# The first attention's softmax: a maximum on VectorE, a bias on GpSimd, and an exponential that reads PSUM

## The chip, the cores and the metric

The kernel runs on one core of one Trainium2 chip. The metric is the device time of one execution in microseconds (us). The core has a matrix engine (TensorE, PE in the profile; its weight loads are PEld), VectorE (DVE), ScalarE (ACT), GpSimd (POOL) and SyncE (SP), which issues most DMAs. Each engine has its own queue and works through it in order; semaphores make one wait for another. TensorE writes its results into PSUM, a small memory of eight banks of 128x512 float32; VectorE and ScalarE read it there, and the other tiles live in SBUF.

## The reference, cut to what matters

The program is an encoder of two layers over 512 tokens of width 1024. The first layer has two groups of eight attention heads, A (grouped queries, width 64) and B (latent attention, width 64 + 32), then an output projection and an MLP. The second layer has a neighbourhood attention and an MLP. The change is in the softmax of the first layer alone:

```python
sc = jnp.einsum('bkgqd,bksd->bkgqs', qblk, kt).astype(jnp.float32) * scale
p = jax.nn.softmax(sc, axis=-1).astype(vt.dtype)
return jnp.einsum('bkgqs,bksd->bkgqd', p, vt)
```

For each head and each block of 128 queries this is a tile of 128x512 scores: scale, subtract the largest of each row, exponentiate, divide by the row's sum, multiply by the values. The scale holds the per-query norm of A's and B's queries too, so it is one number per row (per partition).

## The kernel before

All matrix products are made of float32r parts: a value is split into a high part (ScalarE copies it with rounding) and a low part (VectorE or GpSimd subtracts the high part), and two or three matmuls of the parts are added up in PSUM. So each matmul of a weight costs a ScalarE copy and a VectorE subtraction as well (`chunk`, L202 and L212 and L222), and so does each result that is used again (`split`, L830 and L833; `split_g`, L507 and L508).

The first attention is `attend` (from L961). It goes over 16 heads (8 of A, then two groups of 4 of B) and over 4 query blocks in each, 64 score tiles in all. For one tile, `scores` (L993 and on) does this:

- It takes one of the two PSUM banks of the tag `s` (`sbk`) and issues two matmuls (A) or three (B) into it (L997).
- L1001, VectorE: one custom instruction reads the scores from the bank, adds zero, multiplies by a negative scale, writes the result to the SBUF tile `p`, and keeps the minimum of each row in the tiny tile `t`. A second short instruction reads that accumulator out. Then the bank is free.
- L1003, ScalarE: the exponential of minus `p` plus that minimum, in place in `p`, with the row's sum kept (again a second instruction reads the accumulator out).
- L1004, VectorE: the reciprocal of the sum.
- L1005, GpSimd: `p` times the reciprocal.

Three tiles later `transpose` turns `p` with four TensorE transposes into a PSUM bank `t` (L972), ScalarE copies the high part out (L974) and VectorE the low part (L975). When two query blocks of a head are there, `values` multiplies them with the head's values into the bank `o` (L985), and `fold` adds the halves of the result (L946 on ScalarE, L949 on VectorE). `p` has five buffers, `t` (the tiny tile) six, and the banks `s` and `t` two each.

Beside the heads `step` feeds other work into the program (`fill`): the input projection's later columns (L501 to L503 on TensorE), the projections of B, and the first half of the output projection. Their helpers use GpSimd for low parts (L202) and for the rotary products (L562, L563).

The scales are prepared once: `q_scales` (L707 and on) makes `scA` for A, and `latents` makes `scB` for B (L816).

The order in which the instructions of this part stand in the engines' queues is not written out by hand. A planner takes the program's order as a priority, estimates each instruction's duration and the moment at which its inputs and buffers are there, and sorts the queues. Only a few places hold the program's order (`keep_in_program_order`, `fixed_order` in the second layer). So a changed instruction can change the order of others.

Of the kernel before, what the change touches and what calls it, by code (L numbers as in the profile page):

```python
# [11 lines left out]
AF = mybir.ActivationFunctionType  # L12
ALU = mybir.AluOpType
AX = mybir.AxisListType
PSUM = bass.MemoryType.PSUM

S = 512
D = 1024
P = 128
# [11 lines left out]
def f32(ap):  # L31
    return ap.bitcast(F32)
# [3 lines left out]
def encoder_kernel(ctx: ExitStack, tc: tile.TileContext, ins, out, dbg=None):  # L36
    nc = tc.nc
    PE, ACT, DVE, POOL, SP = nc.tensor, nc.scalar, nc.vector, nc.gpsimd, nc.sync
# [22 lines left out]
    def nm(s):  # L61
        cnt[0] += 1
        return f"{s}_{cnt[0]}"
# [18 lines left out]
    def sbk():  # L82
        return bank("s", 2)

    def stb():
        return bank("t", 2)

    def ob():
        return bank("o", 1)
# [4 lines left out]
    def tiny(n, dt=F32):  # L94
        return tp.tile([P, n], dt, tag=f"ti{n}", name=nm("ti"))

    def keep(shape, dt, name):
        return big.tile(shape, dt, tag=name, name=name)
# [9 lines left out]
    zeros = keep([P, 1], F32, "zeros")  # L108
# [362 lines left out]
    class Fill:  # L471
# [8 lines left out]
        def step(self):  # L480
            try:
                self.credit -= next(self.q[0][1])
            except StopIteration:
                self.q.pop(0)
# [42 lines left out]
    def bcast_cols(col_ap, nparts, bk):  # L527

        for i in range(4):
            PE.transpose(bk[0:nparts, i * P : (i + 1) * P], col_ap(i), ident)  # L530
# [38 lines left out]
    def stats_to_tok(bk, n, name):  # L569

        st = scratch()
        ACT.activation(st[0:n, :], bk[0:n, :], AF.Copy)
        tb = stb()
        for i in range(4):
            PE.transpose(tb[:, i * n : (i + 1) * n], st[0:n, i * P : (i + 1) * P], ident[0:n, 0:n])
        v = keep([P, 4 * n], F32, name)
        v3 = v.rearrange("p (i n) -> p i n", i=4)
        DVE.tensor_tensor(v3, tb[:, 0 : 4 * n].rearrange("p (i n) -> p i n", i=4),
                          r0sq.unsqueeze(2).to_broadcast([P, 4, n]), op=ALU.mult)
        DVE.tensor_scalar(v, v, 1.0, EPS, op0=ALU.mult, op1=ALU.add)  # L580
        y = rsqrt(v, 4 * n)
        DVE.tensor_tensor(v3, y.rearrange("p (i n) -> p i n", i=4),
                          r0.unsqueeze(2).to_broadcast([P, 4, n]), op=ALU.mult)
        return v3
# [17 lines left out]
    def ind2(t):  # L602
        return cst[:, C_I2 + 2 * t : C_I2 + 2 * t + 2]
# [103 lines left out]
    def q_scales():  # L707
        rs = stats_to_tok(hold["stq"], 8, "rsQ")
        sc = keep([P, 4, 8], F32, "scA")
        DVE.tensor_scalar(sc, rs, -0.125, 1.0, op0=ALU.mult, op1=ALU.mult)  # L710
        hold["scA"] = sc


# [46 lines left out]
    for m in range(6):  # L760
# [9 lines left out]
        else:  # L770
            ev_q(m - 2, banks[m])
    q_scales()
    rope_q(0)

# [32 lines left out]
    def latents():  # L807

        b = stb()
        for z in range(2):  # L810
            PE.matmul(b[0:2, :], ind2(z), sqs[z].t[:, 0:512], start=z == 0, stop=z == 1)
        sB = stats_to_tok(b, 2, "rsB")
        for z in range(2):
            sqs[z].free()
        scB = keep([P, 4], F32, "scB")
        DVE.tensor_scalar(scB, sB[:, :, 0], -(96.0 ** -0.5), 1.0, op0=ALU.mult, op1=ALU.mult)  # L816
        bk = stb()
        bcast_cols(lambda i: sB[:, i, 1:2].to_broadcast([P, P]), P, bk)
        hold["skvb"] = Slot(F32)
        ACT.activation(hold["skvb"].t[:, 0:512], bk, AF.Copy)  # L820
        hold["sB"], hold["scB"] = sB, scB
        for s_ in X:
            s_.free()
        yield 1.5
# [116 lines left out]
    def fold(o, e):  # L941

        if e == 0:
            hold["pair"] = scratch()
        a, c, pair = 64 * e, scratch(), hold["pair"]
        ACT.activation(c[0:64, :], o[64:128, :], AF.Copy)  # L946

        def add():
            DVE.tensor_tensor(pair[a : a + 64, :], o[0:64, :], c[0:64, :], op=ALU.add)  # L949
            if e:  # L950
                O.append(Slot())
                soon_a(lambda o=O[-1]: split(pair, o.pair()))

        soon(add)
# [6 lines left out]
    def attend(heads, step):  # L961


        late_t, late_v = [], []

        def transpose(h, i, p):
            if i % 2 == 0:
                h["pt"] = Slot(), Slot()
            h3, l3 = (s_.t.rearrange("p (k q) -> p k q", k=4)[:, :, (i % 2) * P : (i % 2 + 1) * P] for s_ in h["pt"])
            tb = stb()  # L970
            for k in range(4):
                PE.transpose(tb[:, k * P : (k + 1) * P], p[:, k * P : (k + 1) * P], ident)  # L972
            t3 = tb.rearrange("p (k q) -> p k q", k=4)
            ACT.activation(h3, t3, AF.Copy)  # L974
            DVE.tensor_tensor(l3, t3, f32(h3), op=ALU.subtract)  # L975
            if i % 2:
                late_v.append((h, i // 2, h["pt"]))

        def values(h, half, pt):
            if half == 0:  # L980
                h["o"] = ob()
            o = h["o"]
            for k in range(4):
                for n, m in enumerate(pt):
                    PE.matmul(o[:, 256 * half : 256 * half + 256], h["vlhs"](k), m.t[:, 256 * k : 256 * k + 256],  # L985
                              start=k == 0 and n == 0, stop=k == 3 and n == 1, skip_group_check=True)
            for s_ in pt:
                s_.free()
            if half:
                fold(o, h["e"])  # L990
                h["after"]()

        def scores(h, i):  # L993
            s = sbk()
            pl = h["passes"](i)
            for n, (lh, rh) in enumerate(pl):
                PE.matmul(s, lh, rh, start=n == 0, stop=n == len(pl) - 1)  # L997
            h["done"](i)
            t = tiny(4)
            p = pp.tile([P, 512], F32, tag="p", name=nm("p"))  # L1000
            DVE.tensor_tensor_reduce(p, s, zeros.to_broadcast([P, S]), op0=ALU.add, op1=ALU.min, scale=h["scale"](i),  # L1001
                                     scalar=3e38, accum_out=t[:, 1:2])
            ACT.activation(p, p, AF.Exp, bias=t[:, 1:2], scale=-1.0, accum_out=t[:, 2:3])  # L1003
            DVE.reciprocal(t[:, 3:4], t[:, 2:3])  # L1004
            POOL.tensor_scalar(p, p, t[:, 3:4], 1.0, op0=ALU.mult, op1=ALU.mult)  # L1005
            return p

        for h in heads:
            for i in range(4):
                ripe = list(late_v)  # L1010
                p = scores(h, i)
                if len(late_t) == 3:
                    transpose(*late_t.pop(0))
                late_t.append((h, i, p))
                if ripe:
                    values(*late_v.pop(0))
                step(h, i)
        for x in late_t:
            transpose(*x)
            while late_v:  # L1020
                values(*late_v.pop(0))
            fill.run(1.5)
# [68 lines left out]
    fill.add("z", product(w_in, 0, XP, tiles(1152, 256), ev_ckv, three, eng=POOL))  # L1091
    fill.add("z", rotary_key())
    fill.add("z", latents())
    projB(0, False)
    attend(all_heads(), step)
# [633 lines left out]
```

## Time and profile before

| What | us |
|---|---|
| median of three runs | 1184.7 |
| the three runs | 1185.4, 1184.7, 1183.35 |
| span of the profiled execution, first to last instruction | 1184.0 |
| PE busy in the span | 1160.5 (98%) |
| VectorE busy | 883.2 (75%) |
| ScalarE busy | 640.3 (54%) |
| GpSimd busy | 526.1 (44%) |

The time of the profiled execution itself is its span; the runs were timed apart from it. The mean granted clock of TensorE is 0.994 of full speed.

How to read the views. A row of instructions gives the line of the kernel, the engine, the operation, the tiles written and read, their shapes and how many there are; then busy time in us and the mean length of one in ns; then the idle time of the engine just before them, and which instruction's end stopped it. In the timeline a row begins with its start and its length in us, and a bracket gives the idle time before it and what ended it. In the waits a row says which instruction waited for which: us in total, times, the longest. The chain of work that ended last is followed back from the last instruction of the program: at each step to what released it, or to the instruction ahead of it on its engine.

### The profile page before, as it was taken

Reading aid. Unit: us, or ns where it says so; the run is one execution under the profiler, and the core shown is the slowest. Engines: PE = TensorE matmul, PEld = TensorE weight load, DVE = VectorE, ACT = ScalarE, POOL = GpSimd, SP = SyncE. Lnnn points to the kernel's source line nnn. Section 1 sums busy time; section 2 is a strip of 40 time slices with the busy share of each in tenths; the row PEclk is TensorE's granted clock in tenths of the full one; section 3 lists DMA queues with packets and bytes.
Section 4 is the critical chain, followed back from the end, with each engine's and each line's share of the span. In section 5 each row is a group of like instructions: output and inputs, shape, how many; then the busy total and the mean of one; then the engine's idle time right before and its main releaser. Section 6 shows DMA issues by size and latency. Waiting matters only on the chain.

```text
span 1184.0 us, 19784 instructions
## 1 busy us (share of the span) xinstructions
PE 1160.5 (98%) x7128; PEld 1021.2 (86%) x7128; DVE 883.2 (75%) x1514; ACT 640.3 (54%) x1081; POOL 526.1 (44%) x662
## 2 busy tenths in 40 slices
PE   9989999999999999999999999999999999999997
PEld 8667778888899899988998998988889989998895
DVE  5788998878967368786884676667996736778975
ACT  4468676664546247562553565555554624666344
POOL 3267343224562377819602232231376625774710
PEclk9999999999999999999999999999999999999998
DMA  7223225212524723225226464433352341322412
GB/s 244 71 54 92 68 78 134 62 56 77 167 86 134 263 70 90 72 90 165 67 72 178 131 184 126 116 112 109 107 165 76 115 134 55 98 64 89 143 36 71
DMA packets 110145, 128.01 MB, mean 108 GB/s; under 512 B 9075, under 2 KB 86816, under 8 KB 110048
## 3 DMA queue, kind: packets, MB, share of 16 engines
q1 hardware_dynamic: 106992, 119.30, 33.5%
q0 software_dynamic: 2304, 6.31, 2.2%
q8 instruction: 56, 0.92, 0.3%
q10 hardware_dynamic: 752, 1.15, 0.3%
q14 instruction: 41, 0.34, 0.1%
HBM read 104.32 MB, written 6.29 MB: 93 GB/s over the span
## 4 chain that ended last, share of the span: by engine, by line
PE 81%; DVE 4%; ACT 1%; issue 1%; POOL 0%; DVEq 0%; ACTq 0%
PE mm L503 8%; PE mm L501 8%; PE mm L502 8%; PE mm L390 4%; PE mm L389 4%; PE mm L388 4%; PE t L388 3%; PE t L389 3%; PE t L390 3%; PE s L502 2%; PE s L503 2%; PE s L501 2%; PE s L390 2%; PE s L388 2%; PE s L389 2%; PE s L997 2%
## 5 line engine op out<-in xcount | busy, mean ns | idle before, releaser
L309 DVE TENSOR_TENSOR wlo<-a,whi 128x896 fp32r<-128x896 f32 x132 | 161.8, 1230 | 83.7 <-ACT whi L308 82.9
L308 ACT ACTIVATE whi<-a 128x896 fp32r<-128x896 f32 x132 | 125.0, 950 | 155.0 <-PE o L502 45.8
L501 PE MATMUL mm<-a,whi 128*128 128x512 f32 x485 | 195.9, 406 | 0.9 <-DVE a L915 0.7
L503 PE MATMUL mm<-a,wlo 128*128 128x512 f32 x485 | 192.1, 397 | 2.5 <-DVE wlo L202 2.5
L502 PE MATMUL mm<-a,whi 128*128 128x512 f32 x485 | 192.5, 397 | 0.1
L202 DVE TENSOR_TENSOR wlo<-raw,whi 128x1024 fp32r<-128x1024 f32 (+4 forms) x117 | 139.3, 1193 | 66.4 <-ACT whi L212 63.9
L212 ACT ACTIVATE whi<-raw 128x1024 fp32r<-128x1024 f32 (+3 forms) x120 | 116.4, 971 | 92.2 <-PE s L502 39.8
L302 POOL TENSOR_TENSOR a<-a 128x128 f32<-128x128 f32 x132 | 85.1, 645 | 173.3 <-DMA a<-in_ffn_w_up_dram 103.9
L303 POOL TENSOR_TENSOR a<-a 128x256 f32<-128x256 f32 x132 | 120.2, 910 | 10.3
L304 POOL TENSOR_TENSOR a<-a 128x128 f32<-128x128 f32 x132 | 115.1, 872 | 10.3
L503 PEld LDWEIGHTS mm<-a,wlo 128*128 128x128 f32 x485 | 91.7, 189 | 23.7 <-DVE wlo L202 3.4
L501 PEld LDWEIGHTS mm<-a,whi 128*128 128x128 f32 x485 | 91.8, 189 | 20.4 <-PE t L972 0.9
L502 PEld LDWEIGHTS mm<-a,whi 128*128 128x128 f32 x485 | 91.9, 190 | 17.4 <-DVE a L545 0.4
L388 PE MATMUL mm<-a,whi 128*128 128x256 f32 x370 | 103.9, 281 | 0.0
L389 PE MATMUL mm<-a,whi 128*128 128x256 f32 x370 | 103.9, 281 | 0.0
L390 PE MATMUL mm<-a,wlo 128*128 128x256 f32 x370 | 103.7, 280 | 0.0
L1005 POOL TENSOR_SCALAR p<-p,ti 128x512 f32<-128x512 f32 x64 | 46.2, 724 | 92.3 <-DVE ti L1004 81.1
L1430 POOL TENSOR_SCALAR p<-p,ti 128x256 f32<-128x256 f32 x64 | 35.6, 567 | 104.8 <-DVE ti L1429 91.8
L388 PE MATMUL t<-a,whi 128*128 128x256 f32 x264 | 74.2, 281 | 0.0
L389 PE MATMUL t<-a,whi 128*128 128x256 f32 x264 | 74.1, 281 | 0.0
L390 PE MATMUL t<-a,wlo 128*128 128x256 f32 x264 | 73.9, 280 | 0.0
L390 PEld LDWEIGHTS mm<-a,wlo 128*128 128x128 f32 x370 | 69.6, 188 | 0.2 <-DVE wlo L309 0.2
(338 smaller groups left out, 3210.8 us busy)
## 6 DMA issues: line engine op xcount, KB each, us to landing
a<-in_ffn_w_up_dram SPq DMA_DIRECT2D x104, 256.0 KB
raw<-in_ffn_w_down_dram SPq DMA_DIRECT2D x46, 512.0 KB
raw<-in_od_w_qkv_dram SPq DMA_DIRECT2D x64, 128.0 KB
a<-in_ffn_w_down_dram SPq DMA_DIRECT2D x28, 256.0 KB
raw<-in_ffn_w_up_dram SPq DMA_DIRECT2D x12, 512.0 KB
raw<-in_ev_w_in_dram SPq DMA_DIRECT2D x12, 384.0 KB
a<-a SPq DMA_DIRECT2D x18, 256.0 KB
bias<-bx SPq DMA_DIRECT2D x16, 256.0 KB
```

The lines of the kernel that those rows point to most:

```text
L202: z = lambda: (eng or DVE).tensor_tensor(to, src, f32(high), op=ALU.subtract)
L212: ACT.activation(hi[:, 0:m], raw[:, 0:m], AF.Copy)
L303: POOL.tensor_tensor(r[:, 4:6], r[:, 2:3].to_broadcast([P, 2, P]), r[:, 0:7:6], op=ALU.add)
L304: POOL.tensor_tensor(r[:, 7], r[:, 3], r[:, 5], op=ALU.subtract)
L308: ACT.activation(hi[:, 0:896], raw[:, 128:1024], AF.Copy)
L309: DVE.tensor_tensor(lo[:, 0:896], raw[:, 128:1024], f32(hi[:, 0:896]), op=ALU.subtract)
L388: PE.matmul(o, wh, x[:, 0], start=kp == 0 and n in (0, 1, 3, 5), stop=False, skip_group_check=True)
L389: PE.matmul(o, wh, x[:, 1], start=False, stop=False, skip_group_check=True)
L390: PE.matmul(o, wl, x[:, 0], start=False, stop=kp == self.np - 1, skip_group_check=True)
L501: PE.matmul(o, wh, xh, start=first, stop=False)
L502: PE.matmul(o, wh, xl, start=False, stop=False)
L503: PE.matmul(o, wl, xh, start=False, stop=last)
```

## The change

VectorE only takes the maximum of each row of scores, straight from the bank. GpSimd multiplies it by the scale and by minus one, which gives the bias. ScalarE then reads the scores from the bank, and its instruction takes the scale and the bias as two operands per partition. The scales lose their minus sign, because the exponential now takes them as they are. `p` is first written by ScalarE. The bank is last read by ScalarE. The tile `zeros` is no longer read here.

```diff
@@ q_scales
-        DVE.tensor_scalar(sc, rs, -0.125, 1.0, op0=ALU.mult, op1=ALU.mult)
+        DVE.tensor_scalar(sc, rs, 0.125, 1.0, op0=ALU.mult, op1=ALU.mult)
@@ latents
-        DVE.tensor_scalar(scB, sB[:, :, 0], -(96.0 ** -0.5), 1.0, op0=ALU.mult, op1=ALU.mult)
+        DVE.tensor_scalar(scB, sB[:, :, 0], 96.0 ** -0.5, 1.0, op0=ALU.mult, op1=ALU.mult)
@@ scores
             t = tiny(4)
             p = pp.tile([P, 512], F32, tag="p", name=nm("p"))
-            DVE.tensor_tensor_reduce(p, s, zeros.to_broadcast([P, S]), op0=ALU.add, op1=ALU.min, scale=h["scale"](i),
-                                     scalar=3e38, accum_out=t[:, 1:2])
-            ACT.activation(p, p, AF.Exp, bias=t[:, 1:2], scale=-1.0, accum_out=t[:, 2:3])
+            DVE.tensor_reduce(t[:, 0:1], s, axis=AX.X, op=ALU.max)
+            POOL.tensor_scalar(t[:, 1:2], t[:, 0:1], h["scale"](i), -1.0, op0=ALU.mult, op1=ALU.mult)
+            ACT.activation(p, s, AF.Exp, bias=t[:, 1:2], scale=h["scale"](i), accum_out=t[:, 2:3])
             DVE.reciprocal(t[:, 3:4], t[:, 2:3])
             POOL.tensor_scalar(p, p, t[:, 3:4], 1.0, op0=ALU.mult, op1=ALU.mult)
             return p
```

## The prediction

> **What bounds the kernel now.** I read the page first (the span, the chain that ended last), then the busy time in 20 us stretches to find the part that the change touches, then the chain inside that part, and last the waits there.
>
> ```profile
> span 1184.0 us, 19784 instructions
> ...
> PE 81%; DVE 4%; ACT 1%; issue 1%; POOL 0%; DVEq 0%; ACTq 0%
> ```
>
> The chain is TensorE (PE) nearly all the way. The 64 score tiles of the first attention run from 73.8 us to the last scaling at 244.3 us (rows below), and only there can the change act. In the stretches, the fields are length, PE, weight load, VectorE (DVE), ScalarE (ACT), GpSimd (POOL), each in us and count, then granted clock, DMA share and GB/s:
>
> ```profile
> 70.00:90.00 20.00, 17.59 (x90) 13.70 (x88) 16.89 (x46) 15.18 (x32) 10.02 (x13) 0.91 0.18 47
> 90.00:110.00 20.00, 19.10 (x116) 15.83 (x116) 17.16 (x44) 16.20 (x38) 15.39 (x18) 1.00 0.35 100
> 130.00:150.00 20.00, 19.01 (x125) 16.46 (x125) 18.26 (x44) 17.13 (x36) 5.01 (x7) 1.00 0.33 74
> 150.00:170.00 20.00, 18.88 (x115) 16.02 (x116) 18.49 (x46) 15.38 (x35) 9.12 (x12) 1.00 0.29 76
> 190.00:210.00 20.00, 20.00 (x122) 17.15 (x121) 16.76 (x38) 12.79 (x28) 3.34 (x4) 1.00 0.63 168
> ```
>
> The reader sees two halves. From 190 us PE is busy without a gap: nothing that only relieves VectorE can pay there. Up to 170 us PE is idle for 1 to 2.4 us in each 20, and VectorE is at 17 to 18.5 of 20. The chain, from 140 us on (start, us, what), shows VectorE as the engine that ends last there:
>
> ```profile
> 144.09 0.66 DVE p L1001
> 144.75 0.01 DVE ti L1001
> 144.75 0.60 DVE a L975
> 145.36 0.60 DVE a L830
> ```
>
> So in this stretch a shorter VectorE instruction counts, but by little: L1001 takes 0.66 us of the queue, its neighbours 0.60.
>
> **The change, part by part.** Durations, from the groups of instructions between 68 and 250 us by form (busy us, mean ns, idle before); then a group of the whole trace, and two lines by themselves (shortest/median/longest ns, first and last start):
>
> ```profile
> L1005 POOL TENSOR_SCALAR p<-p,ti 128x512 f32<-128x512 f32 x64 | 46.2, 724 | 92.3 <-DVE ti L1004 81.1 <-DVE ti L166 4.1 <-PE s L997 3.6
> L1003 ACT ACTIVATE p<-p,ti 128x512 f32<-128x512 f32 x64 | 46.1, 720 | 12.2 <-DVE ti L1001 11.6
> L1001 DVE CUSTOM_DVE_ANT_0 p<-s,zeros,scB 128x512 f32<-128x512 f32 x32 | 23.7, 744 | 3.4 <-PE s L997 2.9 <-POOL p L1005 0.3
> L202 POOL TENSOR_TENSOR wlo<-raw,whi 128x512 fp32r<-128x512 f32 x9 | 12.7, 1409 | 5.2 <-ACT whi L222 4.1 <-ACT whi L212 1.1
> L833 ACT ACTIVATE a<-sc 128x512 fp32r<-128x512 f32 x13 | 8.2, 627 | 3.2 <-DVE sc L949 1.3 <-DVE sc L566 0.9 <-DVE sc L881 0.9
> L1001 DVE DVE_READ_ACCUMULATOR2_ANT ti<- 128x1 f32 x64 | 5.3, 83 | 0.0
> L507 ACT ACTIVATE a<-mm,gT 128x512 fp32r<-128x512 f32 x5 | 3.4, 681 | 0.0
> L833 ACT ACTIVATE a<-mm 128x512 fp32r<-128x512 f32 x4 | 2.4, 595 | 0.0
> ```
>
> ```profile
> L546 DVE COPY hT<-t 128x512 f32<-128x512 f32 x8 | 5.5, 682 | 0.0
> ```
>
> ```profile
> L1005 POOL TENSOR_SCALAR p<-p,ti x64: 688/696/1653, 77.6 to 244.3; 128x512 f32<-128x512 f32 x64
> ```
>
> ```profile
> L1430 POOL TENSOR_SCALAR p<-p,ti x64: 471/482/1697, 641.8 to 808.1; 128x256 f32<-128x256 f32 x64
> ```
>
> *VectorE.* 64 custom reductions (744 ns, with an 83 ns accumulator read each) go, 64 maxima over a 128x512 tile in PSUM come. No plain reduction stands in this trace. The nearest row is the copy out of PSUM of the same shape, 682 ns (L546); the bounds are 595 ns (the ScalarE copy out of PSUM) and 827 (744 + 83, if a maximum also needs its accumulator read). I take 682. In the queue, where instructions overlap a little, that is the step from 0.66 to the 0.60 us of L975: 0.06 us a tile, 64 x 0.06 = 3.8 us of VectorE in all. At 64 tiles in 171 us about 25 lie inside the VectorE-bound 90 to 157 us: 1.5 us. Not all of it reaches the end, since chain pieces of PE and ScalarE lie between: I count **-1.2 us**, from 0 to -4.
>
> [...]
>
> *GpSimd.* 64 tiny multiplications on 128x1 come. L1005 (512 wide, median 696) and L1430 (256 wide, 482) lie 214 ns apart, so a width of 1 is about 482 - 214 = 268 ns. Bounds: nothing beyond the handover, and 482. I take 270: 64 x 0.27 = 17 us of POOL. The longest of each, 1653 and 1697, show that such an instruction can be held up for a microsecond. POOL is not on the chain and has the room on average (15.39 of 20 at the fullest). But its queue is in order: a bias stands behind whatever POOL runs, an L202 of 1409 ns or the 724 ns L1005 of an earlier tile, itself waiting for a reciprocal. Behind the bias stand the same L1005 and L202, and for them wait the transposes (L972) and the next weights.
>
> *ScalarE.* The exponential reads PSUM, not SBUF: 595 against 627, 32 ns less. It has a second operand per partition (the scale): 681 against 595, 86 ns more. So 720 - 32 + 86 = 774 ns, 64 x 54 ns = 3.5 us more of ScalarE, which has at least 2.9 us free in every 20 before: no charge, except in the latency below.
>
> *The bank.* This is the part that can cost. There are two score banks (`sbk`). Before, a bank is free when VectorE has read it; after, when ScalarE has finished the exponential. The steady case before, in the timeline, with a VectorE-to-GpSimd handover from further on:
>
> ```profile
> 176.08 0.75 DVE L1001 CUSTOM_DVE_ANT_0 p<-s,zeros,scB 128x512 f32<-128x512 f32 x1 [0.22 <-PE s L997]
> 176.76 0.08 DVE L1001 DVE_READ_ACCUMULATOR2_ANT ti<- 128x1 f32 x1
> 176.90 0.72 ACT L1003 ACTIVATE p<-p,ti 128x512 f32<-128x512 f32 x1
> ...
> 178.29 0.87 PE L997 MATMUL s<-a,a 96*128 96x512 f32 x3
> ...
> 181.77 0.40 PE L997 MATMUL s<-a,a 96*128 96x512 f32 x1
> ```
>
> ```profile
> 241.03 0.15 DVE L1004 RECIPROCAL ti<-ti 128x1 f32<-128x1 f32 x1
> ...
> 241.35 0.70 POOL L1005 TENSOR_SCALAR p<-p,ti 128x512 f32<-128x512 f32 x1 [1.38 <-DVE ti L1004]
> ```
>
> Before: free 0.76 us after the start of L1001, exponential finished after 1.54. After: 0.68 + 0.17 (handover, 241.18 to 241.35) + 0.27 + 0.06 (handover to ScalarE, 176.84 to 176.90) + 0.77 = 1.95. So the exponential ends **0.41 us later** and the bank is held **1.19 us longer**. In this steady case the cover is wide: the scores that reuse the bank start at 181.77, 3.7 us after an exponential that would end at 178.03. Where PE issues scores in a burst there is none:
>
> ```profile
> 73.80 0.75 DVE L1001 CUSTOM_DVE_ANT_0 p<-s,zeros,scA 128x512 f32<-128x512 f32 x1 [0.15 <-DVE scA L710]
> ...
> 74.59 0.73 ACT L1003 ACTIVATE p<-p,ti 128x512 f32<-128x512 f32 x1 [1.46 <-DVE ti L1001]
> 74.61 0.76 PE L997 MATMUL s<-a,a 128*128 128x512 f32 x2 [2.39 <-DVE ti L1001]
> ```
>
> The third scores wait for the first bank. PE has nothing else in front in its queue, so this one moves by the whole 1.19: **+1.2 us**. How often the like happens is in the waits (us in total, times, longest):
>
> ```profile
> PEld s L997 <- DVE ti L1001: 4.7, 5, 2.8
> ...
> PEld o L985 <- DVE a L975: 4.3, 11, 1.0
> ...
> PE s L997 <- DVE ti L1001: 2.9, 2, 2.4
> ...
> PEld t L972 <- POOL p L1005: 1.3, 4, 0.5
> ...
> PE t L972 <- DVE ti L1004: 0.5, 2, 0.3
> ```
>
> Seven waits of PE for a bank, one of them the first burst. The other six would cost 6 x 1.19 = 7.1 us if the order stayed. But the order here is not written out: a planner sorts the queues by its own durations and can put projection matmuls where a bank is not free. I charge one in three, **+2.4**. The transposes wait six times for the scaled tile or its reciprocal, which now comes 0.41 us later: 2.5 at most, a third again, **+0.8**.
>
> Sum: -1.2 + 1.2 + 2.4 + 0.8 = **+3.2 us** on the span of 1184.0. The median of the runs, 1184.7, lies 0.7 above that span, and I add the sum to it: 1187.9.
>
> **The rivals.** *The relief of VectorE wins (faster).* For it: VectorE ends the chain from 140 to 157, and PE waits 4.3 us in 11 pieces for L975, which stands behind L1001 in VectorE's queue. Against it: only 0.06 us a tile. If a maximum is as short as 595 ns and the planner keeps all bank waits covered, -4 of VectorE time and none of the charges except the start: -4 + 1.2 = -2.8, so 1181.9; it decides as soon as the six bank waits grow by under 0.3 us each.
>
> *Both hide (no change).* The filler matmuls cover the banks, PE stays the bound: -1.2 + 1.2, 1184.7.
>
> *GpSimd becomes the bound of each tile (much slower).* From 90 to 110 us POOL is busy 15.39 of 20; seven or eight biases add 2.0, and each may first sit out an L202 of 1.4 us. Then exponentials come late on a queue where L974 stands behind them, and VectorE and PE follow. All six waits in full (7.1), the transposes in full (2.5), the start (1.2) and one more slow-clock window (1.7, next): 1184.7 + 12.5 = 1197.2.
>
> The slow clock is seen in two stretches of the same fields:
>
> ```profile
> 71.77:75.18 3.41, 1.02 (x5) 0.51 (x4) 2.99 (x14) 1.93 (x3) 0.00 (x0) 1.00 0.03 9
> 75.18:78.59 3.41, 3.41 (x10) 2.60 (x9) 2.21 (x8) 2.56 (x8) 0.69 (x1) 0.50 0.00 0
> ```
>
> After 3.41 us with PE idle for 2.4 of them, the granted clock is 0.50 for 3.41 us, worth 1.7 us of PE. The start moved by 1.2 keeps PE idle to 75.8, inside the slow window, so I expect one such window as before. [...]
>
> *The maximum costs as much as what it replaces.* At 827 ns VectorE gains nothing; the sum without its term is +4.4, 1189.1, inside the forecast's range.
>
> **How the numbers follow.** Forecast (bank and handover cost a little, +2.4 to +9): 0.45. GpSimd bound: 0.10. Both hide, within 2.4 us: 0.18. VectorE's relief wins: 0.27. About 0.2%, 2.4 us, is what a measurement can tell from no change. So slower 0.55, same 0.18, faster 0.27. Range 1180.5 to 1197: the low end is -4.2 (all of the VectorE bound), the high end the GpSimd case; about 0.2 lies outside.
>
> **What the changed profile would show.** The maximum between 595 and 744 ns; the exponential near 774; the bias near 270 and rows of waits "ACT p <- POOL ti" in the place of the 11.6 us for L1001. Scores waiting for ACT instead of DVE, more than 7.6 us in all, would show the forecast; less, with VectorE's waits for PE rising, the faster rival. The queues' order will differ from before, and if PE's gaps from 250 us on change as well, the planner has moved more than I followed, and the sum is wrong by a term that I have not named.

## The result, and the profile after

The changed kernel takes 1202.9 us in the median (1201.7 to 1205.2, four runs). The kernel before took 1184.7 beside it (1183.35 to 1185.4). The ratio is 1.0159, with a 95% interval of 1.0145 to 1.0173: slower by 18.8 us by the ratio (the medians lie 18.2 apart), where the forecast said 3.2 and the range ended at 12. Below, a ratio becomes "us over the kernel before" by (ratio - 1) x 1184.7; a ratio's interval is about 2 us to each side.

The page of the changed kernel, its span and the chain that ended last:

```profile
span 1200.5 us, 19791 instructions
...
PE 81%; DVE 8%; ACT 4%; POOL 3%; issue 3%; DMA 1%; SPq 0%; POOLq 0%; DVEq 0%; ACTq 0%
```

VectorE, ScalarE and GpSimd now hold 15% of the chain instead of 5%. The stretches of the changed kernel (length, then PE, weight load, VectorE, ScalarE, GpSimd in us and count, granted clock, DMA share, GB/s):

```profile
70.00:90.00 20.00, 16.95 (x86) 12.65 (x86) 15.50 (x33) 14.94 (x30) 13.20 (x20) 1.00 0.30 85
90.00:110.00 20.00, 17.88 (x109) 14.31 (x108) 15.86 (x32) 16.27 (x36) 14.65 (x23) 1.00 0.17 43
130.00:150.00 20.00, 17.89 (x97) 13.90 (x96) 15.80 (x43) 10.87 (x22) 7.14 (x10) 1.00 0.32 86
150.00:170.00 20.00, 17.56 (x110) 14.38 (x108) 17.10 (x34) 14.92 (x32) 9.35 (x15) 1.00 0.35 86
190.00:210.00 20.00, 17.91 (x105) 15.18 (x104) 16.89 (x30) 12.89 (x25) 9.86 (x14) 1.00 0.39 100
...
70.00:270.00 200.00, 181.58 (x1011) 144.53 (x1011) 153.01 (x306) 135.80 (x278) 98.31 (x153) 0.99 0.26 70
```

and the last of these stretches in the kernel before:

```profile
70.00:270.00 200.00, 193.58 (x1091) 158.35 (x1090) 172.09 (x394) 142.98 (x296) 77.78 (x93) 0.99 0.29 79
```

In the stretch from 190 to 210 us, which had no gap, PE now idles for 2.1 us. From 70 to 270 us PE idles for 200 - 181.58 = 18.4 us instead of 6.4, and VectorE is less busy too (153.0 us instead of 172.1), so VectorE isn't the bound. By 270 us PE has done 80 matmuls fewer; at the mean of 193.58 / 1091 = 0.177 us each that is an estimate of 14.2 us. A later mark is surer: the first matmul of L388, in a product far behind the attention, starts at 354.3 us instead of 336.2, 18.1 us later, and the program's last instruction ends 16.5 us later. So the whole loss arises before that mark.

The changed instructions, each by its line (shortest/median/longest ns, first and last start):

```profile
L1001 DVE TENSOR_REDUCE ti<-s x64: 661/682/693, 70.6 to 259.9; 128x1 f32<-128x512 f32 x64
...
L1002 POOL TENSOR_SCALAR ti<-ti,scA x32: 258/268/1226, 75.2 to 167.4; 128x1 f32<-128x1 f32 x32
...
L1003 ACT ACTIVATE p<-s,ti,scA x32: 762/778/797, 75.5 to 167.7; 128x512 f32<-128x512 f32 x32
```

In the median the prices were right: 682, 270 and 774 ns were forecast. The waits of the changed kernel between 68 and 270 us (us in total, times, longest) show what was not:

```profile
ACT p L1003 <- POOL ti L1002: 40.4, 40, 2.7
...
DVE ti L1004 <- ACT p L1003: 18.1, 35, 1.4
PEld s L997 <- ACT p L1003: 13.5, 23, 1.6
...
PE s L997 <- ACT p L1003: 7.0, 11, 1.3
...
PEld o L985 <- ACT a L974: 6.3, 13, 1.1
PEld o L985 <- DVE a L975: 4.7, 7, 1.4
...
PE o L985 <- DVE a L975: 3.1, 4, 1.2
...
PEld t L972 <- POOL p L1005: 0.9, 3, 0.4
```

against these of the kernel before:

```profile
ACT p L1003 <- DVE ti L1001: 11.6, 15, 1.5
...
DVE ti L1004 <- ACT p L1003: 1.2, 5, 0.3
...
PEld o L985 <- ACT a L974: 0.8, 4, 0.2
```

The rows of PE and of its weight load (PEld) must not be added, since they show the same stalls twice. The stall at 74.61 us in the kernel before stands in both, as 2.39 and as 2.82 us, and in the changed kernel each of PE's eleven waits for a bank goes with one of the weight load's 23. So a score bank is waited for 23 times instead of 5. PE itself idles 7.0 us for it instead of 2.9, the weight load 13.5 instead of 4.7. In the other twelve the weight load is late and PE shows no wait for a bank, so I take PE's row as a low estimate of the price and the weight load's as a high one. (The expectations below add the two rows, as the prediction did: 7.6 us in 7 waits before, 20.5 in 34 after.) ScalarE stands idle at the exponential 40 times, for 40.4 us instead of 11.6. How one wait becomes the next is seen in the timeline of the changed kernel (start, us; a bracket gives the idle time before and what ended it):

```profile
176.04 0.68 DVE L1001 TENSOR_REDUCE ti<-s 128x1 f32<-128x512 f32 x1
...
176.82 0.27 POOL L1002 TENSOR_SCALAR ti<-ti,scB 128x1 f32<-128x1 f32 x1 [1.01 <-DVE ti L1001]
...
177.12 0.78 ACT L1003 ACTIVATE p<-s,ti,scB 128x512 f32<-128x512 f32 x1
...
180.83 0.88 DVE L830 TENSOR_TENSOR a<-sc,a 128x512 fp32r<-128x512 f32 x1
...
181.15 0.70 POOL L1002 TENSOR_SCALAR ti<-ti,scB 128x1 f32<-128x1 f32 x1
...
181.88 0.78 ACT L1003 ACTIVATE p<-s,ti,scB 128x512 f32<-128x512 f32 x1 [0.76 <-POOL ti L1002]
...
182.86 0.69 DVE L1001 TENSOR_REDUCE ti<-s 128x1 f32<-128x512 f32 x1
...
183.12 0.69 POOL L1005 TENSOR_SCALAR p<-p,ti 128x512 f32<-128x512 f32 x1 [1.27 <-PE mm L503]
...
183.64 0.60 PE L972 MATMUL t<-cst,p 128*128 128x128 f32 x4
183.78 0.27 POOL L1002 TENSOR_SCALAR ti<-ti,scB 128x1 f32<-128x1 f32 x1
...
184.09 0.78 ACT L1003 ACTIVATE p<-s,ti,scB 128x512 f32<-128x512 f32 x1 [0.84 <-POOL ti L1002]
...
184.86 0.59 ACT L974 ACTIVATE a<-t 128x512 fp32r<-128x512 f32 x1
```

The first tile runs as forecast: 177.12 + 0.78 - 176.04 = 1.86 us from the maximum's start to the exponential's end (forecast 1.95). In the last one the maximum ends at 183.55, but GpSimd is in the scaling of another tile until 183.8. ScalarE idles for 0.84 us. Behind the exponential in its queue stands the copy L974, whose transposes were done at 184.24; it starts at 184.86, 0.62 us late, and VectorE's L975 and the values wait for it. The middle tile shows a bias that takes 0.70 us in place of 0.27, beside a VectorE subtraction with two inputs from SBUF (180.83 to 181.71). This is so in the whole trace: 17 of the 64 biases took 0.63 to 1.31 us, and each of them overlapped a VectorE instruction with two SBUF inputs; the other 47 took less than 0.32 us, and none of them did.

### The profile page after: what moved, and what is told of

Read it like the earlier page. It is cut to its first block, busy times and chain, and to the rows that moved or that the text cites. A ratio compares the mean times of both kernels' runs of the same rounds, so it can differ in the third digit from the quotient of the medians.

```text
span 1200.5 us, 19791 instructions
## 1 busy us (share of the span) xinstructions
PE 1164.2 (97%) x7128; PEld 1019.9 (85%) x7128; DVE 881.2 (73%) x1450; ACT 644.5 (54%) x1081; POOL 546.2 (45%) x726
## 4 chain that ended last, share of the span: by engine, by line
PE 81%; DVE 8%; ACT 4%; POOL 3%; issue 3%; DMA 1%; SPq 0%; POOLq 0%; DVEq 0%; ACTq 0%
PE mm L501 8%; PE mm L503 8%; PE mm L502 8%; PE mm L390 4%; PE mm L389 3%; PE mm L388 3%; PE t L388 3%; PE t L389 3%; PE t L390 3%; PE s L502 3%; PE s L503 3%; PE s L501 3%; PE s L390 2%; PE s L388 2%; PE s L389 2%
## 5 line engine op out<-in xcount | busy, mean ns | idle before, releaser
L303 POOL TENSOR_TENSOR a<-a 128x256 f32<-128x256 f32 x132 | 118.2, 895 | 10.3
L501 PEld LDWEIGHTS mm<-a,whi 128*128 128x128 f32 x485 | 91.2, 188 | 24.1 <-DVE a L508 2.8
L502 PEld LDWEIGHTS mm<-a,whi 128*128 128x128 f32 x485 | 91.4, 188 | 16.7
L388 PE MATMUL mm<-a,whi 128*128 128x256 f32 x370 | 103.9, 281 | 0.0
L388 PE MATMUL t<-a,whi 128*128 128x256 f32 x264 | 74.2, 281 | 0.0
L389 PEld LDWEIGHTS mm<-a,whi 128*128 128x128 f32 x370 | 69.6, 188 | 0.2
```

What stands on the lines that cost most here:

```text
L303: POOL.tensor_tensor(r[:, 4:6], r[:, 2:3].to_broadcast([P, 2, P]), r[:, 0:7:6], op=ALU.add)
L388: PE.matmul(o, wh, x[:, 0], start=kp == 0 and n in (0, 1, 3, 5), stop=False, skip_group_check=True)
L389: PE.matmul(o, wh, x[:, 1], start=False, stop=False, skip_group_check=True)
L501: PE.matmul(o, wh, xh, start=first, stop=False)
L502: PE.matmul(o, wh, xl, start=False, stop=False)
```

## The experiments

### Bank or step: each half alone

Two theories stood at first. **Bank:** the score bank is held until the exponential has ended. **VectorE's queue:** the exponential is late, and the reciprocal, waiting for it at the head of VectorE's queue, holds back what is behind. Four kernels separate the halves.

e1: the kernel before, and GpSimd multiplies the finished bias by 1. The bank is freed early.

```diff
-  scalar=3e38, accum_out=t[:, 1:2])
+  scalar=3e38, accum_out=t[:, 0:1])
+  POOL.tensor_scalar(t[:, 1:2], t[:, 0:1], 1.0, 1.0, op0=ALU.mult, op1=ALU.mult)
```

> Two theories. Bank: the loss comes from the score bank that is held to the end of the exponential, so TensorE waits for it (7.6 us in 7 waits before, 20.5 in 34 after). VectorE's queue: the loss comes from the longer way over GpSimd, which makes the reciprocal late, and VectorE stands still in front of it (1.2 us in 5 waits before, 18.1 in 35 after) with the transposes' low parts behind it. Here the bank is freed early as before, and only the hop over GpSimd is added (GpSimd multiplies the bias by 1). Bank expects 1184 to 1189 us. VectorE's queue expects 1195 to 1203, with over 12 us of waits at the reciprocal.

e2: the kernel before, with the exponential reading the bank (and a second, positive scale tile); the bias still comes from VectorE's custom instruction.

```diff
-  ACT.activation(p, p, AF.Exp, bias=t[:, 1:2], scale=-1.0, accum_out=t[:, 2:3])
+  ACT.activation(p, s, AF.Exp, bias=t[:, 1:2], scale=h["pos"](i), accum_out=t[:, 2:3])
```

> VectorE makes the bias as before (its copy of the scores in p is not used), no hop over GpSimd, but the exponential reads the bank with a positive scale, so the bank is held to its end. Bank expects 1195 to 1203 us, with over 15 us of TensorE's waits for the exponential. VectorE's queue expects 1184 to 1189, with under 5 us of waits at the reciprocal.

e3: the changed kernel, with the bias on VectorE.

```diff
-  POOL.tensor_scalar(t[:, 1:2], t[:, 0:1], h["scale"](i), -1.0, op0=ALU.mult, op1=ALU.mult)
+  DVE.tensor_scalar(t[:, 1:2], t[:, 0:1], h["scale"](i), -1.0, op0=ALU.mult, op1=ALU.mult)
```

> The changed kernel with the bias made by VectorE itself, right behind the maximum. The handovers and the 0.40 us on GpSimd become about 0.16 to 0.25 us on VectorE, whose queue gets 64 short instructions more. Bank expects most of the loss to stay, 1196 to 1203 us. VectorE's queue expects the waits at the reciprocal to halve, 1188 to 1195.

e4: the changed kernel without the reciprocal; GpSimd multiplies by the sum itself, so the division is left out.

```diff
-  DVE.reciprocal(t[:, 3:4], t[:, 2:3])
-  POOL.tensor_scalar(p, p, t[:, 3:4], 1.0, op0=ALU.mult, op1=ALU.mult)
+  POOL.tensor_scalar(p, p, t[:, 2:3], 1.0, op0=ALU.mult, op1=ALU.mult)
```

> The changed kernel without the reciprocal: GpSimd multiplies by the sum, so the softmax is not normalised. VectorE has nothing in its queue that waits for the exponential, and 64 instructions of 0.16 us fewer. Bank expects 1197 to 1203 us, with TensorE's waits for the exponential unchanged near 20 us. VectorE's queue expects 1180 to 1190.

| Run | us | ratio (95%) | us over before |
|---|---|---|---|
| e1, step on GpSimd alone | 1195.6 | 1.0096 (1.0081 to 1.0112) | 11.4 |
| e2, bank alone | 1193.0 | 1.0071 (1.0054 to 1.0088) | 8.4 |
| e3, change with bias on VectorE | 1190.2 | 1.0048 (1.0033 to 1.0063) | 5.7 |
| e4, change without reciprocal | 1202.0 | 1.0147 (1.0132 to 1.0162) | 17.4 |

e1 and e3 came out in the ranges of the second theory, e4 in that of the first, and e2 in neither. e4 gives back nothing that could be told from the changed kernel, so the reciprocal's place in VectorE's queue is not the cause there. Both halves cost, and 11.4 + 8.4 = 19.8 is the 18.8 within the intervals. That the sum fits so well is partly luck. At the mark of L388, in one profiled execution each, e1 is 9.3 us late and e2 4.1, together 13.4 of the changed kernel's 18.1; a further 2.8 us of e2's loss arises behind the mark, in a part that the edit doesn't touch. So some 5 us may come only where both halves meet.

e2 also missed what the bank theory had expected of its waits, over 15 us. Its waits for the bank are shorter in sum than the 4.7 and 2.9 us of the kernel before (L1003 is the scores there, L1009 the exponential):

```profile
PEld s L1003 <- ACT p L1009: 3.7, 9, 1.2
...
PE s L1003 <- ACT p L1009: 1.4, 3, 0.8
```

So the price of the bank half is measured, but the path on which it is paid there isn't shown. With the bias on VectorE two thirds of the loss are gone, though the bank is still held to the exponential's end. So the larger part is a step of a quarter of a microsecond on GpSimd. Where no bank hangs on it, the waits of e1 name its way (L1003 is the step there, L1004 the exponential, L1005 the reciprocal):

```profile
ACT p L1004 <- POOL ti L1003: 38.4, 36, 3.2
...
DVE ti L1005 <- ACT p L1004: 15.6, 22, 2.6
PEld o L985 <- DVE a L975: 8.6, 13, 3.0
```

ScalarE idles for 38.4 us, VectorE behind it for 15.6, and the weight load waits for L975 8.6 us (4.3 before). With the bias from VectorE, ScalarE's idle time is half of that; e2 and e3:

```profile
ACT p L1009 <- DVE ti L1007: 18.3, 23, 2.3
```

```profile
ACT p L1003 <- DVE ti L1002: 18.6, 19, 2.7
```

### Which engine, and the place of the exponential

e5: the changed kernel, with the exponential (then the reciprocal and the scaling) placed behind the transposes of the same step; the exponential is held there by `keep_in_program_order`. e6 is the same edit in the kernel before.

```diff
-  p = scores(h, i)
+  p, finish = scores(h, i)    # finish: exponential, reciprocal, scaling
   if len(late_t) == 3:
       transpose(*late_t.pop(0))
+  finish()
```

> The changed kernel, with the exponential and what follows it placed in the program behind the transposes of the same step, and held there in ScalarE's queue. Queue-order theory: the exponential loses because it stands at the head of ScalarE's in-order queue before its bias from GpSimd has come, with copies of transposes behind it; placed behind them it waits less: ScalarE's wait for GpSimd at the exponential falls from 40.4 us to under 20, TensorE's waits for the scores' bank do not grow, and the time falls from 1202.9 to 1190 to 1196. Handover theory: the bias's way over GpSimd is paid by the bank wherever the exponential stands; it now ends later still, TensorE waits more for the scores' bank than the 20.5 us of the changed kernel, and the time is 1201 to 1210.

> The kernel before with the same placing of the exponential behind the transposes: the control for e5. Queue-order and handover theory both: the bank is free before the exponential, and VectorE's result is there in time, so little changes, 1183 to 1189. If any other order of the queues costs or gains some us by itself, this run moves by as much as the one above, and neither can be read as an effect of the hop.

e7: the changed kernel, with ScalarE making the bias.

```diff
-  POOL.tensor_scalar(t[:, 1:2], t[:, 0:1], h["scale"](i), -1.0, op0=ALU.mult, op1=ALU.mult)
+  ACT.activation(t[:, 1:2], t[:, 0:1], AF.Copy, scale=h["neg"](i))
```

> The changed kernel with the bias made by ScalarE itself, one short instruction ahead of the exponential, instead of by GpSimd. If the crossing to GpSimd is what costs (queue-order and handover theory both), the time is that of the bias on VectorE, 1188 to 1194, although ScalarE gets 64 more instructions of some 0.2 us. If any further link between maximum and exponential costs as much, on whatever engine, it is 1200 to 1206.

e8: as e1, with the step on VectorE (`DVE.tensor_scalar`).

> The kernel before with one short VectorE instruction that multiplies the bias by 1, between the minimum and the exponential; the bank is freed early as before. It stands beside the same step on GpSimd, 1195.6. If the crossing to GpSimd costs: 1184 to 1188 here. If any further link in the chain costs the same, 1193 to 1198. If it gets faster than 1184, the planner's order alone is worth some us.

| Run | us | ratio (95%) | us over before |
|---|---|---|---|
| e5, change, exponential behind the transposes | 1206.2 | 1.0175 (1.0150 to 1.0199) | 20.7 |
| e6, before, the same | 1188.1 | 1.0023 (1.0007 to 1.0038) | 2.7 |
| e7, change, bias on ScalarE | 1195.5 | 1.0087 (1.0064 to 1.0110) | 10.3 |
| e8, before, step on VectorE | 1189.6 | 1.0039 (1.0026 to 1.0052) | 4.6 |

e8 against e1: the same link costs 4.6 on VectorE and 11.4 on GpSimd; e8's 1189.6 is a little more than the 1184 to 1188 that I had expected. e7 missed by 1.5 us and lies between both: with the bank held, the bias costs 5.7 in all on VectorE, 10.3 on ScalarE, 18.8 on GpSimd. e5 came out as the handover theory had it. But its row shows that the edit didn't do what it was for (L1005 is the exponential):

```profile
ACT p L1005 <- POOL ti L1002: 40.7, 37, 3.2
```

ScalarE idles as long as in the changed kernel, 40.7 against 40.4 us: behind the same step's transposes the exponential is still too early. So e5 takes nothing away and can't judge the queue-order theory, for which it was made.

### GpSimd's own queue

f1: the changed kernel without the reciprocal and the scaling (the two lines go, and with them the division). f2: the same two lines taken from the kernel before.

> The changed kernel without reciprocal and without GpSimd's multiplication of the exponentials (left out: the normalisation; the transposes read the exponentials as they are). Beside the next run it tells what the change costs when GpSimd has no long instruction and no wait for the sums around its biases. GpSimd's queue theory (the bias comes late because it stands in order behind the scaling and other products of GpSimd, and they behind it): the change costs over the next run what it costs with the bias on VectorE, 3 to 9 us. Theory of the crossing alone: the hop costs wherever GpSimd's queue stands, 14 to 20 us over the next run.

> The kernel before without reciprocal and without GpSimd's multiplication (left out: the normalisation): the control for the run above. Both theories: 1180 to 1186, as GpSimd's scaling has slack of some us before the transposes.

f3: e3, and GpSimd makes the bias once more into a tile that nothing reads.

```diff
+  u = tiny(1)
+  POOL.tensor_scalar(u, t[:, 0:1], h["scale"](i), -1.0, op0=ALU.mult, op1=ALU.mult)
```

> The changed kernel with the bias made on VectorE (1190.2 so far), and GpSimd makes the same bias once more into a tile that nothing reads. Nothing waits for it, but it stands at the head of GpSimd's queue until the maximum is there. If the cost of the hop is that the bias holds back what stands behind it on GpSimd (scaling, low parts), it stays: 1197 to 1204. If the cost is that the bias itself comes late to the exponential, it is gone: 1188 to 1193.

f4: the changed kernel, with the scaling on VectorE (`DVE.tensor_scalar(p, p, t[:, 3:4], ...)`).

> The changed kernel with the multiplication of the exponentials moved from GpSimd to VectorE: the whole computation stays, GpSimd keeps the biases and its other products. GpSimd's queue theory: TensorE's waits for the scores' bank fall from 20.5 us to under 12, and the time to 1190 to 1198, unless VectorE's 64 further instructions of 0.3 to 0.7 us take the gain. Theory of the crossing alone: the waits for the bank stay, 1201 to 1210.

| Run | us | ratio (95%) | us over before |
|---|---|---|---|
| f1, change without scaling | 1195.3 | 1.0096 (1.0076 to 1.0117) | 11.4 |
| f2, before without scaling | 1180.7 | 0.9972 (0.9961 to 0.9982) | -3.3 |
| f3, e3 and an unread copy | 1195.3 | 1.0093 (1.0078 to 1.0108) | 11.0 |
| f4, change, scaling on VectorE | 1208.5 | 1.0213 (1.0187 to 1.0239) | 25.2 |

With no scaling on GpSimd at all the change costs 11.4 + 3.3 = 14.7 us, within the 14 to 20 of the crossing alone, and f4 keeps the bank waits (weight load 12.5 us, PE 6.8), with a scaling of 479 ns in the median on VectorE. In f1 and in f4 ScalarE still idles at the exponential; first f1, then f4:

```profile
ACT p L1003 <- POOL ti L1002: 33.0, 34, 4.0
```

```profile
ACT p L1003 <- POOL ti L1002: 33.1, 34, 2.4
...
PEld s L997 <- ACT p L1003: 12.5, 22, 1.6
...
PE s L997 <- ACT p L1003: 6.8, 11, 1.4
```

So the scaling that stands on GpSimd beside the bias isn't the main cause. Work on GpSimd isn't free, though: f3 costs 5.3 us over e3, and nothing waits for its copy. It fell between the two expectations, and its mechanism stays open.

### The wait at ScalarE's head, taken away

What all kernels so far with the bias on GpSimd share is ScalarE's idle time at the exponential, 33 to 41 us. The next runs take that wait away and leave the step in. The exponential goes one whole tile back: `finish` of the last tile comes behind the next tile's scores and the transposes that follow them. g1 is e1 with this edit, g2 the changed kernel, g3 the kernel before.

```diff
   p, finish = scores(h, i)
   if len(late_t) == 3:
       transpose(*late_t.pop(0))
+  if pend:
+      pend.pop()()
+  pend.append(finish)
```

> The kernel before with the step on GpSimd in front of the exponential (1195.6 so far, the bank freed early), and the exponential held one tile later in ScalarE's queue: behind the next tile's scores and the copy of the transposes that follow them. ScalarE's-head theory: the step costs because ScalarE stands idle at the exponential until GpSimd's result comes (38.4 us), with copies behind it; now the result is there long before, that wait falls under 10 us, and the time to within 3 us of the control with the same order (the third run here). Theory of the crossing alone: the chain is as long as before, so the time stays 8 to 12 us above the control.

> The changed kernel with the same later exponential. ScalarE's wait for GpSimd falls under 10 us by both theories, but the bank is now held over the next tile. ScalarE's-head theory: the waits behind ScalarE go, and the bank's remain or grow, 1196 to 1206. Bank theory (most of the 18 us is the bank's): TensorE's waits for the bank grow from 20.5 to over 30 us and the time is 1208 or more.

> The kernel before with the same later exponential: the control. Both theories: VectorE's result is there in time anyway, and three tiles lie between the scores and the transposes, two of which stay: 1182 to 1190.

| Run | us | ratio (95%) | us over before |
|---|---|---|---|
| g1, step on GpSimd, exponential a tile later | 1187.9 | 1.0029 (1.0019 to 1.0039) | 3.4 |
| g2, change, exponential a tile later | 1196.3 | 1.0102 (1.0087 to 1.0117) | 12.1 |
| g3, before, exponential a tile later | 1192.5 | 1.0068 (1.0049 to 1.0088) | 8.1 |

g1 (L1003 is the step, L1006 the exponential), then g2 and g3 (L1005 the exponential, L1007 the scaling):

```profile
PEld t L972 <- POOL p L1008: 10.5, 18, 1.6
...
ACT p L1006 <- POOL ti L1003: 4.6, 4, 2.0
```

```profile
PEld s L997 <- ACT p L1005: 5.9, 18, 0.7
...
ACT p L1005 <- POOL ti L1002: 4.1, 6, 1.7
```

```profile
PEld t L972 <- POOL p L1007: 11.5, 16, 2.5
...
PE t L972 <- POOL p L1007: 6.4, 8, 2.3
```

The step is still there, but ScalarE's wait for it falls from 38.4 to 4.6 us and its price is gone: g1 takes 8.0 us less than e1 and lies 4.7 us below its control. That is more than the 3 us to either side that I had expected, and why it lies below is not known. In the changed kernel the same edit gives back 6.7 us, where the bank theory had expected 1208 us or more. The order has a price of its own, which I had not expected of g3: the transposes have lost a tile, and there the weight load waits for `p` 11.5 us and PE 6.4.

The last runs give that tile back: the transposes come four tiles behind the scores (`len(late_t) == 4`; `step` adds the output projection at n == 36). h1 is g3 with this, h2 is g2, h3 the kernel before with this alone.

> The kernel before with the exponential one tile later in ScalarE's queue, as in the control of the last three runs (1192.5), and the transposes four tiles behind the scores instead of three (five buffers of p as before; the step that adds the output projection moves by one tile with them). In the control TensorE waited 17.9 us for p at the transposes, where it waits 3.0 in the kernel before. If that missing tile is what the later exponential cost, these waits fall under 6 us and the time is 1180 to 1187; if the later order itself costs, 1190 to 1195.

> The changed kernel with both: exponential one tile later, transposes four tiles behind (1196.3 with the first alone, of which TensorE waited 17.2 us for p at the transposes). ScalarE's-head theory with the bank as a part of its own: the waits for p go, the bank's 6.8 us stay, 1187 to 1193, that is 4 to 9 us above the run before this one. If the hop has a price that no order takes away, it is 1196 or more.

> The kernel before with the transposes four tiles behind the scores and nothing else: the control for the two runs above. p has one spare buffer less, so the minimum can wait for a buffer of p: 1183 to 1192 by both theories.

| Run | us | ratio (95%) | us over before |
|---|---|---|---|
| h1, before, both edits | 1183.7 | 0.9993 (0.9980 to 1.0005) | -0.8 |
| h2, change, both edits | 1190.8 | 1.0055 (1.0036 to 1.0074) | 6.5 |
| h3, before, transposes later alone | 1187.4 | 1.0020 (1.0005 to 1.0034) | 2.4 |

h2 (L1005 is the exponential):

```profile
ACT p L1005 <- POOL ti L1002: 8.5, 8, 1.8
PEld s L997 <- ACT p L1005: 8.4, 18, 1.4
...
PE s L997 <- ACT p L1005: 2.7, 6, 1.0
```

With the order fitted to it, the change costs 6.5 + 0.8 = 7.3 us, in the 4 to 9 expected. So the 18.8 us are two things, known roughly by their size. Some 11 us are the step on GpSimd, paid through ScalarE's idle time in front of its result: a later exponential takes both away. Some 6 to 8 us are left where that wait is halved (5.7 in e3, 8.4 in e2) or shorter still (7.3 here), and no order here took them away. All three hold the bank to the exponential's end, but only a part of the 7.3 is seen as waiting for it: the weight load waits 8.4 us where h1 has 3.6, PE itself 2.7 where h1 has 2.4. No version of the change is faster than the kernel before; h1, which has only the new order, is equal to it.

What stays open: on which path the rest of those 6 to 8 us is paid, and no run has the step on GpSimd alone in the order of h1; f3's 5.3 us, some of which may be in e1's 11.4 as well, though g1, with the same step on GpSimd, shows nothing of it; and differences of up to 5 us between kernels whose queues are sorted anew (e6 and h3 moved by 2.7 and 2.4 without any new work, g1 lies 4.7 below its control). Why the planner doesn't move the exponential back by itself was not tried.

## Why the prediction was wrong, point by point

- **Prices of the instructions:** right in the median, within 4 ns. The maximum took 682 ns, as long as the copy that I had taken for it. The rival in which the maximum costs 827 ns fell with it. What was missed is the spread of the bias: 268 in the median, but up to 1307, so that the 64 took 25.6 us of GpSimd instead of 17.
- **VectorE's relief, -1.2:** not seen. VectorE's work in the 90 to 110 us stretch fell by 1.3 us, yet the waits for L975 at the values didn't fall (weight load 4.3 us before, 4.7 now; PE 1.2 and 3.1): VectorE now waits for ScalarE 18.1 us at the reciprocal.
- **The latency, 0.41 and 1.19 us:** right for a tile whose bias meets a free GpSimd (1.86 us against 1.95).
- **The start, +1.2:** not there. The maximum needs no scale and runs at 70.6, three us earlier. The exponentials still come later than before, and so do the third scores (78.11 instead of 74.61), but PE takes projections first and starts the scores without waiting for a bank. Here are the second exponential and the third scores:

```profile
76.29 0.77 ACT L1003 ACTIVATE p<-s,ti,scA 128x512 f32<-128x512 f32 x1
...
78.11 0.63 PE L997 MATMUL s<-a,a 128*128 128x512 f32 x2
```

- **The slow clock:** one window, as expected, but not at the start. The granted clock is 1.00 from 75.18 to 78.59 us, and 0.55 from 113.65 to 117.06, behind 3.41 us in which PE idled for 1.74 (110.24 to 113.65). From 71.77 to 75.18 it idled for 1.42, and the clock stayed at 1.00. The much slower rival's second window did not come. The 1.7 us in its sum were an estimate from the one window of the kernel before (0.50 for 3.41 us); no run shows what would bring a second.
- **The bank, +2.4: mis-sized, and by the wrong count.** I took seven waits from the old profile, but two rows showed the same stalls, so there were five. I charged one in three because "a planner sorts the queues by its own durations and can put projection matmuls where a bank is not free". It did that at the start; over the whole attention the count rose to 23, PE's own waits by 4.1 us and the weight load's by 8.8. Holding the bank costs 8.4 us alone (e2); the prediction has no term for the part of it that isn't a wait for the bank.
- **"POOL is not on the chain and has the room on average" and "no charge, except in the latency": this is the step that failed.** GpSimd had the room. But the exponential stood at the head of ScalarE's queue, and 40 times ScalarE idled there until the bias came (40.4 us), with the copies, VectorE's subtractions and the values behind. I charged a third of 2.5 us for it, at the transposes, which don't show it (six waits before, three after). The runs give it 11 us: 11.4 in e1, of which g1 gives 8.0 back, to below its control.
- **The rivals:** the one with 0.10 named that way ("exponentials come late on a queue where L974 stands behind them, and VectorE and PE follow") and said 1197.2. It was right in the consequence and 5.7 us short. GpSimd isn't the bound: it is busy for 14.65 us of 20 in the fullest of the stretches shown. The faster rival and the neutral one had no support: every run with the change in it is slower than the kernel before. So the direction of the forecast was right, and its reason, the bank, is the smaller part of the loss.
- **The signs to look for:** scores waiting for ScalarE, "more than 7.6 us in all", came as 20.5 in the same doubled count. PE's gaps also reach past 250 us, which I had named as the sign of a missing term: the attention itself lasts longer, with its last maximum at 259.9 us, where the last scaling was at 244.3.

## What to carry to other kernels

When a step is moved to another engine, ask what stands behind its consumer in the consumer's queue, and what idle time a late result makes there: the moved step's own duration and the free share of its engine don't answer that. Waits counted in the old profile are no bound for the new one: here 5 stalls became 23. And if such a step must be taken, try a later place for the consumer in its queue, and give the tile back that this costs further on. Here the later place alone took the step's price from 11 us to none over a control in the same order, and both together took the whole change from 18.8 us to 7.3.

## What the runs showed of the hardware

A multiplication on 128x1 wasn't free on any of the three engines that made it. With a scale per partition GpSimd took 268 ns in the median (the changed kernel), ScalarE 292 (e7) and VectorE 204 (e3); with constants GpSimd took 192 (g1) and VectorE 142 (e8). The rows of g1 and e7:

```profile
L1003 POOL TENSOR_SCALAR ti<-ti x64: 182/192/1103, 73.3 to 243.6; 128x1 f32<-128x1 f32 x64
```

```profile
L1008 ACT ACTIVATE ti<-ti,snA x32: 278/292/321, 76.0 to 162.3; 128x1 f32<-128x1 f32 x32
```

On GpSimd the longest was four to six times the median: 1307 ns against 267 in the changed kernel, 1103 against 192 in g1. In the changed kernel each of the 17 long ones (0.63 to 1.31 us) overlapped a VectorE instruction with two SBUF inputs. A plain maximum over 512 scores in PSUM took as long as a copy of a tile of that shape out of PSUM: 682 ns in the median (L1001, changed kernel) and 682 in the mean (L546, kernel before).
